# A hybrid decoder step on one core: x of the head groups and B brought to tokens on the partitions by VectorE's 32x32 transposes and a trip through DRAM

## The chip, the core and the metric

The kernel runs on one core of a Trainium2 chip. The metric is the device time of one execution in microseconds (us). The engines are TensorE (PE, with PEld for its weight loads), VectorE (DVE), ScalarE (ACT), GpSimd (POOL) and SyncE (SP, which here only issues DMAs). Each engine works through its own list of instructions in order.

## The reference

One step of a decoder layer with two parallel head groups, followed by a convolutional feed-forward part, for 256 prompt tokens and 64 sample tokens (8 sequences of 8):

```python
h = rms_norm(x, p["norm_mix_pre"])
proj = h @ p["w_in"]                       # columns: u | v | z | x,B,C | dt
gate_out, chunk_v = chunk_spatial_gate(a_u, a_v, ...)
ssm_out, new_ssm, new_ssm_conv = ssd_mixer(z, xbc, dt_raw, ...)
mix = jnp.concatenate([gate_out, ssm_out], axis=-1) @ p["w_out"]
x = x + rms_norm(mix, p["norm_mix_post"])
f, new_ffn_conv = conv_ffn(rms_norm(x, p["norm_ffn_pre"]), ...)
x = x + rms_norm(f, p["norm_ffn_post"])
```

The change lies in the state-space part (`ssd_scan`), which works on 32 heads of 64 values in four groups, a state of 128 values, and chunks of 128 tokens. With x, B, C after the convolution and silu:

```python
xdt = (x * dt[..., None])
cb = jnp.einsum("bctgn,bcsgn->bctsg", cc, bc)
y_diag = jnp.einsum("bctsgr,bcsgrp->bctgrp", cb[..., None] * decay, xdt)
states = jnp.einsum("bcsgn,bcsgr,bcsgrp->bcgrpn", bc, decay_states, xdt)
y_off = jnp.einsum("bctgn,bcgrpn,bctgr->bctgrp", cc, states_in, jnp.exp(da_cs))
y = y + d_skip[:, None] * xs
```

The sums over s in `y_diag` and `states` run over tokens, so x and B are needed with tokens on the partitions; the projection and the convolution leave them with channels on the partitions.

## The kernel before

All activations lie transposed: channels on the 128 partitions, the 320 tokens along the free axis (256 prompt, then 64 sample tokens). Every weight matrix is streamed once in slabs of 128x1024 float32 (512 KB). `slab` loads a slab on SP's queue (L118, `wraw`), ScalarE rounds it to `whi` (L124), VectorE computes the rest `wlo` (L125), and TensorE makes three products for each 128x128 block (L153 to L155: high by high, high by the low part of the activations, low by high), 24 products of 320 columns to a slab. `wraw`, `whi` and `wlo` have three buffers each.

Work between the slabs is written as generators: `project` (an input projection) and `chunk_out` (a part of the output projection) call `tick()` at slab edges, which takes the next step of the first generator in `bg`. A scheduler then decides the order of each engine's instructions from priorities and readiness; `first()` and `high_priority` raise a priority.

The order around the change: projections of v; then B (`conv_proj(B0, ...)` into `bT`), C (`cT`) and the first x (`heads_in(0)`); then four groups of the gate with `chunk_out` 0 to 3; then the pool `sd` opens and the state scan begins. It is run by `ssd(g)` for g = 0 to 3, beside `heads_in(g)`, `chunk_out` and `heads_out(g)`, whose evacuation first finishes `ssd(g)`. Inside `ssd(g)`:

- `load_state` brings the sample sequences' states (`st`, 256 KB each, six buffers) in on SP's queue; `load_sums` brings cumulated decays (`cs`, three buffers).
- `by_token` (L393) is a TensorE transpose of a 128x128 block of x or B into a PSUM bank. For the prompt it takes `xs[:, j]` for two chunks c; for the samples `fourfold` (L397) first copies 32 tokens four times beside each other on ScalarE, and the copy is transposed. B is treated likewise, once, before the first group (L775 to L786): prompt into `btok`, samples into `bsp` with a high and a low part.
- `times` (L824) multiplies the transposed x by dt into `xdt` (prompt and samples) or `xq` (samples with decay), reading PSUM.
- `decayed` (L830, POOL) gives `xde`, from which `s1_ps` (L876) is the state after the first chunk.
- `cb_ps` (L856 to L859) are the products of B and C, `yo_ps` (L887) those of C and the old states, `up_ps` (L904) the states' updates, `y_ps` (L983) the outputs, `fin_ps` (L1011) the last state.

## Time and profile before

| | us |
|---|---|
| runs, median of 3 | 1779.38 (1778.97 to 1780.19) |
| profiled execution, its span | 1779.7 |
| TensorE busy | 1770.5 |
| VectorE busy | 1168.0 |
| ScalarE busy | 819.5 |
| POOL busy | 273.5 |

The profiler names engines and lines: L393 is line 393 of the kernel. A group of instructions is shown as line, engine, operation, output <- inputs, partitions x elements and count, then busy time and the mean duration in ns, then the idle time of the engine just before and what ended it. A row of waits reads: who waited, for whom, us in total, times, the longest. A timeline row reads: start, duration, engine, line, operation. Matmuls are pipelined, so durations of neighbours overlap and TensorE's busy time does not say that it works at its peak.

### The profile page before, as it was taken

To read this page: it belongs to the slowest core of one execution; us is meant where nothing else is said; L and a number is where in the kernel's file an instruction comes from. 1 tells how busy PE (TensorE), PEld (TensorE's weight loads), DVE (VectorE), ACT (ScalarE), POOL (GpSimd) and SP (SyncE) were. 2 spreads that over 40 slices of the span, in tenths; PEclk is the share of its full clock that TensorE was granted. 3 is DMA by queue.
4 is the path that set the end of the run, shared out by engine and by line. 5 is a ranking of instruction groups with operands and counts; after the bars stand their busy time and mean duration, and the time that the engine had idled before them with its cause. 6 is when DMAs were issued, how large, how long until landed. Compare 5 with 4: busy or idle time off the path is not lost.

```text
span 1779.7 us, 30655 instructions
## 1 busy us (share of the span) xinstructions
PE 1770.5 (99%) x11933; PEld 1715.7 (96%) x11933; DVE 1168.0 (66%) x1999; ACT 819.5 (46%) x1195; POOL 273.5 (15%) x602
## 2 busy tenths in 40 slices
PE   9999999999999999999999999999999999999998
PEld 7789999999999998999999999999999999999998
DVE  7549764656977768677865464756656575656575
ACT  5434555334564547445545333343434343433445
POOL 1202200000331313103121011110102020101004
PEclk9999999999999999999999999999999999999999
DMA  7546645456665665554554545545545545454543
GB/s 260 163 148 177 189 128 154 153 153 188 216 190 190 181 207 168 168 171 145 180 156 146 157 149 151 155 148 152 157 144 156 150 150 155 150 150 155 147 154 107
DMA packets 214417, 289.91 MB, mean 163 GB/s; under 512 B 16384, under 2 KB 143744, under 8 KB 214080
## 3 DMA queue, kind: packets, MB, share of 16 engines
q1 hardware_dynamic: 202544, 268.74, 49.6%
q10 hardware_dynamic: 10016, 14.16, 2.2%
q0 software_dynamic: 1712, 5.05, 1.0%
q8 instruction: 94, 1.54, 0.4%
q14 instruction: 51, 0.42, 0.1%
HBM read 273.08 MB, written 14.82 MB: 162 GB/s over the span
## 4 chain that ended last, share of the span: by engine, by line
PE 97%; DVE 1%; ACT 0%; DMA 0%; issue 0%; POOL 0%; POOLq 0%; ACTq 0%; DVEq 0%
PE ps L153 19%; PE ps L155 19%; PE ps L154 19%; PE pd L153 10%; PE pd L155 10%; PE pd L154 10%; PE ps_v L144 7%; PE y_ps L983 1%; PE up_ps L904 0%; PE yo_ps L887 0%; PE sg L731 0%; PE xt_ps L393 0%; DMA cs<-dacs_d 0%; PE x1p L1278 0%; PE tsum L296 0%
## 5 line engine op out<-in xcount | busy, mean ns | idle before, releaser
L125 DVE TENSOR_TENSOR wlo<-wraw,whi 128x1024 fp32r<-128x1024 f32 (+1 forms) x476 | 582.5, 1224 | 432.4 <-ACT whi L124 430.1
L124 ACT CAST whi<-wraw 128x1024 fp32r<-128x1024 f32 (+1 forms) x475 | 494.8, 1042 | 729.9 <-PE ps L154 392.1
L153 PE MATMUL ps<-h_hi,whi 128*128 128x320 f32 x2268 | 704.0, 311 | 0.0
L154 PE MATMUL ps<-h_lo,whi 128*128 128x320 f32 x2268 | 702.7, 310 | 0.0
L155 PE MATMUL ps<-h_hi,wlo 128*128 128x320 f32 x2268 | 702.2, 310 | 0.0
L153 PEld LDWEIGHTS ps<-h_hi,whi 128*128 128x128 f32 x2268 | 426.2, 188 | 2.6 <-issue 1.6
L154 PEld LDWEIGHTS ps<-h_lo,whi 128*128 128x128 f32 x2268 | 426.3, 188 | 0.7
L155 PEld LDWEIGHTS ps<-h_hi,wlo 128*128 128x128 f32 x2268 | 426.2, 188 | 0.0
L155 PE MATMUL pd<-fhi,wlo 128*128 128x320 f32 x704 | 218.2, 310 | 0.0
L153 PE MATMUL pd<-fhi,whi 128*128 128x320 f32 x704 | 218.2, 310 | 0.0
L154 PE MATMUL pd<-flo,whi 128*128 128x320 f32 x704 | 218.2, 310 | 0.0
L153 PE MATMUL pd<-ohi,whi 128*128 128x320 f32 x448 | 139.4, 311 | 0.0
L155 PE MATMUL pd<-ohi,wlo 128*128 128x320 f32 x448 | 138.7, 310 | 0.0
L154 PE MATMUL pd<-olo,whi 128*128 128x320 f32 x448 | 138.7, 310 | 0.0
L153 PEld LDWEIGHTS pd<-fhi,whi 128*128 128x128 f32 x704 | 132.1, 188 | 0.0
L154 PEld LDWEIGHTS pd<-flo,whi 128*128 128x128 f32 x704 | 132.1, 188 | 0.0
L155 PEld LDWEIGHTS pd<-fhi,wlo 128*128 128x128 f32 x704 | 132.1, 188 | 0.0
L1180 POOL COPY ptf<-pad 128x2 f32<-128x2 f32 x88 | 21.0, 239 | 603.7 <-DVE pad L1168 603.0
L249 DVE TENSOR_TENSOR acc_ffn<-acc_ffn,pd 128x320 f32<-128x320 f32 (+1 forms) x161 | 77.5, 482 | 37.8 <-PE pd L155 36.5
L153 PEld LDWEIGHTS pd<-ohi,whi 128*128 128x128 f32 x448 | 84.1, 188 | 1.4 <-issue 1.0
L154 PEld LDWEIGHTS pd<-olo,whi 128*128 128x128 f32 x448 | 84.1, 188 | 0.3
L155 PEld LDWEIGHTS pd<-ohi,wlo 128*128 128x128 f32 x448 | 84.1, 188 | 0.1
(328 smaller groups left out, 1867.9 us busy)
## 6 DMA issues: line engine op xcount, KB each, us to landing
wraw<-in_ffn_w_up SPq DMA_DIRECT2D x176, 512.0 KB, 3.7
wraw<-in_w_in SPq DMA_DIRECT2D x140, 512.0 KB, 3.8
wraw<-in_ffn_w_down SPq DMA_DIRECT2D x88, 512.0 KB, 3.4
wraw<-in_w_out SPq DMA_DIRECT2D x64, 512.0 KB, 3.4
st<-in_state_ssm SPq DMA_DIRECT2D x32, 256.0 KB, 3.9
out_ssm_state_sample<-st ACTq DMA_DIRECT2D x30, 256.0 KB, 3.4
cs<-dacs_d SPq DMA_DIRECT2D x16, 320.0 KB, 4.7
xr<-in_xT SPq DMA_DIRECT2D x4, 640.0 KB, 4.0
```

The costliest lines, as they stand in the source:

```text
L124: rounded[:] = [act.copy(hi, raw).ins]
L125: dve.tensor_tensor(out=lo, in0=raw, in1=hi.bitcast(F32), op=ALU.subtract)
L144: made = pe.matmul(out, xi, w[g][wi], start=first and begins, stop=last and ends)
L153: pe.matmul(ps, whi, xhi, start=first, stop=False)
L154: pe.matmul(ps, whi, xlo, start=False, stop=False)
L155: return pe.matmul(ps, wlo, xhi, start=False, stop=last).ins
L249: added_last[:] = [dve.tensor_tensor(out=acc[:, nb, ts], in0=acc[:, nb, ts], in1=ps[:, ts], op=ALU.add).ins]
L983: pe.matmul(ps[64 * i:64 * i + 64, cols], w(hl), x(hl, m, cpx), tile_position=(0, 64 * i), **flags)
L1180: pool.tensor_copy(ptf[:, k, :], pad[:, 256:258])
```

## The change

No TensorE transposes remain for x and B. `to_tokens` takes a tile with channels on the partitions and, for each part of the tokens (128, 128, 64), lets VectorE transpose its 32x32 blocks (two instructions of 128x512 and one of 128x256 for a tile), then ScalarE's queue issues four writes of it, one for each 32 partitions, into a DRAM buffer with tokens as rows: 12 writes for a tile, five tiles (B and four x), 60 writes. The columns of such a row are in the order (i j f), i the block of partitions, j the tile's block, f the 32 channels.

Reads come back on SP's queue: two of 256 KB for the prompt and eight of 64 KB for the samples (`fourfold` now reads the same 32 rows four times) for each tile, 50 in all. They land in `room()`, tiles that share the three buffers of `cs`. `in_order` turns the columns' order while B is copied to `btok` and `bsp`; `times` does it while multiplying by dt, in two instructions (r = 0, 1) where one stood, reading SBUF.

B and the first x are turned right after their projections. x of group g+1 is turned at the end of `ssd(g)`, behind its products of y in the code. The loads of the states come after the reads of the prompt's x, the products of B and C now stand ahead of everything else that TensorE does in a group, and `state_of_prompt` holds what stood after the first samples' x.

```diff
--- before.py
+++ after.py
@@ -339,6 +339,8 @@
 
     dacs_d = dr.tile([NH, NT + NS], F32, name="dacs_d")
     tot_d = dr.tile([NH, NB], F32, name="tot_d")
+    b_d = dr.tile([NT, 512], F32, name="b_d")
+    x_d = [dr.tile([NT, 512], F32, name=f"x_d{i}") for i in range(4)]
 
 
     hp = ctx.enter_context(tc.tile_pool(name="hp", bufs=1))
@@ -388,14 +390,25 @@
 
     TOK = ((0, P), (P, P), (NP, NS))
 
-    def by_token(ps, x, c):
-
-        pe.transpose(ps, x[:, P * c:P * c + P], ident)
-
-    def fourfold(out, x, i):
-
-        act.copy(out.rearrange("p k (q t) -> p k q t", q=4), x[:, :, NP + 32 * i:NP + 32 * i + 32].unsqueeze(2).to_broadcast([P, 4, 4, 32]))
+    def to_tokens(room, x, rows):
+
+        for o, n in TOK:
+            t = room(o)[:, :4 * n].rearrange("p (s j f) -> p s j f", j=4, f=32)
+            dve.transpose(out=t, in_=x[:, :, o:o + n].rearrange("p j (s t) -> p s j t", t=32))
+            for i in range(4):
+                act.dma_start(rows[o:o + n, P * i:P * i + P].rearrange("(s t) f -> t s f", t=32),
+                              t[32 * i:32 * i + 32].rearrange("p s j f -> p s (j f)"))
+
+    def fourfold(out, rows, i):
+
+        src = rows[NP + 32 * i:NP + 32 * i + 32]
+        for q in range(4):
+            sp.dma_start(out[32 * q:32 * q + 32], src)
         return out
+
+    def in_order(ap):
+
+        return ap.rearrange("p (i j f) -> p j i f", j=4, f=32)
 
     with ExitStack() as mctx:
         op = mctx.enter_context(tc.tile_pool(name="op", bufs=1))
@@ -749,9 +762,12 @@
             conv_proj(B0, 16, lambda j: bT[:, j, :], rooms[0])
             conv_proj(C0, 20, lambda j: cT[:, j, :], rooms[1])
             bg.append(tasks)
+            turned = op.tile([P, 4, NT], F32, tag="xs", name="turned", bufs=2).rearrange("p j n -> p (j n)")
+            to_tokens(lambda o: turned[:, 4 * o:], bT, b_d)
             x0 = heads_in(0, rooms[0])
             finish(normed)
             uf = gate_up(0)
+            to_tokens(lambda o: turned[:, 4 * o:], x0, x_d[0])
             for g in range(4):
                 res = []
                 mix = gate_mix(g, uf, res)
@@ -772,18 +788,20 @@
             cb, cms = shared[:, :NT + NS], shared[:, NT + NS:].rearrange("p (b i) -> p b i", b=NB)
             pool.tensor_copy(cb[:NS, :NS], ident[:NS, :NS])
             pool.tensor_copy(cb[NS:, NT:], ident[NS:, NS:])
-            for c in range(4):
-                ps = misc("bt_ps")
-                b4 = bT if c < 2 else fourfold(sd.tile([P, 4, P], F32, tag="xde", name="b4", bufs=2), bT, c - 2)
-                for g in range(4):
-                    by_token(ps[:, P * g:P * g + P], b4[:, g], c if c < 2 else 0)
-                if c < 2:
-                    act.copy(btok[:, c, :], ps)
-                else:
-                    b = bsp[:, c - 2]
-                    act.copy(b, ps)
-                    for rs in (slice(32, 64), slice(96, P)):
-                        dve.tensor_tensor(out=b[rs], in0=ps[rs], in1=b[rs].bitcast(F32), op=ALU.subtract)
+            def room():
+                return sd.tile([P, 2, NT], F32, tag="cs", name="xt", bufs=3).rearrange("p i n -> p (i n)")[:, :512]
+
+            for c in range(2):
+                b = room()
+                sp.dma_start(b, b_d[P * c:P * c + P])
+                act.copy(btok[:, c, :].rearrange("p (j i f) -> p j i f", j=4, f=32), in_order(b))
+            for c in range(2):
+                b4 = fourfold(room(), b_d, c)
+                b = bsp[:, c]
+                act.copy(b.rearrange("p (j i f) -> p j i f", j=4, f=32), in_order(b4))
+                for rs in (slice(32, 64), slice(96, P)):
+                    h = b[rs].rearrange("p (j i f) -> p j i f", j=4, f=32)
+                    dve.tensor_tensor(out=h, in0=in_order(b4[rs]), in1=h.bitcast(F32), op=ALU.subtract)
 
             def by_head(ap):
                 return ap.rearrange("p (h d) -> p h d", d=64)
@@ -816,13 +834,15 @@
                     sp.dma_start(cs, dacs_d[h0 + 2 * j:h0 + 2 * j + 2, o:o + NT].unsqueeze(0).broadcast_to([P, 2, NT]))
                     return cs
 
-                sts = [load_state(i) for i in range(3)]
-
                 xdt = sd.tile([P, 3, 512], F32, tag="xdt", name="xdt", bufs=1)
-                def times(out, ps, c, at=slice(0, P), h=slice(0, 8)):
-                    n = h.stop - h.start
-                    dve.tensor_tensor(out=by_head(out), in0=by_head(ps),
-                                      in1=dt[at, c, h0 + h.start:h0 + h.stop].unsqueeze(2).to_broadcast([at.stop - at.start, n, 64]), op=ALU.mult)
+                def times(out, x, c, at=slice(0, P), h=slice(0, 8)):
+                    n, m = at.stop - at.start, (h.stop - h.start) // 2
+                    to = out.rearrange("p (j r i f) -> p r j i f", j=m, r=2, i=2)
+                    of = x.rearrange("p (r i j f) -> p r j i f", r=2, i=2, j=4)[:, :, h.start // 2:h.stop // 2]
+                    by = dt[at, c, h0 + h.start:h0 + h.stop].rearrange("p (j r) -> p r j", r=2)
+                    for r in range(2):
+                        dve.tensor_tensor(out=to[:, r], in0=of[:, r],
+                                          in1=by[:, r].unsqueeze(2).unsqueeze(3).to_broadcast([n, m, 2, 32]), op=ALU.mult)
 
                 xsp = sd.tile([P, 2, 512], F32R, tag="xsp", name="xsp", bufs=1)
                 def decayed(i, c):
@@ -832,25 +852,31 @@
                     return xde
 
                 def x_of_samples(i):
-                    ps = misc("xt_ps")
-                    x4 = fourfold(sd.tile([P, 4, P], F32, tag="xde", name="x4", bufs=2), xs, i)
-                    for j in range(4):
-                        by_token(ps[:, P * j:P * j + P], x4[:, j], 0)
+                    x4 = fourfold(room(), x_d[g], i)
                     xq = sd.tile([P, 512], F32, tag="xde", name="xq", bufs=2)
-                    times(xq, ps, 3 + i)
+                    times(xq, x4, 3 + i)
                     act.copy(xsp[:, i], xq)
                     dve.tensor_tensor(out=xsp[64:, i], in0=xq[64:], in1=xsp[64:, i].bitcast(F32), op=ALU.subtract)
                     for r in range(2):
                         at = slice(64 - 64 * r + 32 * i, 96 - 64 * r + 32 * i)
-                        times(xdt[at, 2, 256 * r:256 * r + 256], ps[at, 256 * r:256 * r + 256], 2, at, slice(4 * r, 4 * r + 4))
-
-                for c in range(2):
-                    ps = misc("xt_ps")
-                    for j in range(4):
-                        by_token(ps[:, P * j:P * j + P], xs[:, j], c)
-                    times(xdt[:, c, :], ps, c)
-                    if c == 0:
-                        x0d = decayed(0, 0)
+                        times(xdt[at, 2, 256 * r:256 * r + 256], x4[at], 2, at, slice(4 * r, 4 * r + 4))
+
+                s1 = sd.tile([P, 512], F32, tag="s1", name="s1", bufs=1)
+
+                def x_of_prompt(c):
+                    x = room()
+                    sp.dma_start(x, x_d[g][P * c:P * c + P])
+                    times(xdt[:, c, :], x, c)
+
+                def state_of_prompt(x0d):
+                    ps = misc("s1_ps")
+                    pe.matmul(ps, btok[:, 0, bs], x0d, start=True, stop=True)
+                    act.copy(s1, ps)
+
+                x_of_prompt(0)
+                x0d = decayed(0, 0)
+                x_of_prompt(1)
+                sts = [load_state(i) for i in range(3)]
                 ps = misc("cb_ps")
                 for c in range(2):
                     pe.matmul(ps[:, P * c:P * c + P], bT[:, g, P * c:P * c + P], cT[:, g, P * c:P * c + P],
@@ -872,10 +898,7 @@
                 x_of_samples(0)
                 yield
 
-                ps = misc("s1_ps")
-                pe.matmul(ps, btok[:, 0, bs], x0d, start=True, stop=True)
-                s1 = sd.tile([P, 512], F32, tag="s1", name="s1", bufs=1)
-                act.copy(s1, ps)
+                state_of_prompt(x0d)
 
                 ps_yo = misc("yo_ps")
 
@@ -1002,6 +1025,8 @@
                             products(j - 1)
                         yield
 
+                if g < 3:
+                    to_tokens(lambda o: room(), x_of[g + 1], x_d[g + 1])
                 x1d = decayed(1, 1)
                 pool.tensor_tensor(out=by_head(s1), in0=by_head(s1),
                                    in1=dec[:, 2, h0:h0 + 8].unsqueeze(2).to_broadcast([P, 8, 64]), op=ALU.mult)
```

## The prediction

> **What bounds the kernel now.** First the page of the profile: busy times, and the chain that ended last by engine.
>
> ```profile
> PE 1770.5 (99%) x11933; PEld 1715.7 (96%) x11933; DVE 1168.0 (66%) x1999; ACT 819.5 (46%) x1195; POOL 273.5 (15%) x602
> ...
> PE 97%; DVE 1%; ACT 0%; DMA 0%; issue 0%; POOL 0%; POOLq 0%; ACTq 0%; DVEq 0%
> ```
>
> TensorE is busy for 99% of the span and makes up 97% of the chain. An average hides stages, so next the busy times by stretches (columns: us, then PE, PEld, DVE, ACT and POOL busy with instruction counts, clock, DMA share, GB/s), the last row the whole state-scan part that the change touches:
>
> ```profile
> 465.00:486.00 21.00, 21.00 (x147) 19.52 (x146) 20.92 (x37) 10.96 (x19) 8.05 (x14) 1.00 0.80 251
> ...
> 420.00:740.00 320.00, 318.85 (x2325) 298.74 (x2324) 246.57 (x418) 184.72 (x341) 80.85 (x101) 1.00 0.61 192
> ```
>
> There too TensorE, at a granted clock of 1.00, idles 1.2 us of 320, even in the stretch where VectorE has no gap (20.92 of 21.00). So a TensorE instruction taken away is time taken away, unless a new wait fills it. How far the others run ahead is in the waits of ScalarE, and in three casts of one quiet stretch:
>
> ```profile
> ACT whi L124 <- PE ps L154: 392.1, 186, 4.5
> ...
> 138.78 1.05 ACT L124 CAST whi<-wraw 128x1024 fp32r<-128x1024 f32 x1 [2.43 <-PE ps L154]
> 142.30 1.05 ACT L124 CAST whi<-wraw 128x1024 fp32r<-128x1024 f32 x1 [2.47 <-PE ps L154]
> ```
>
> ScalarE's cast of a weight slab mostly waits until TensorE gives a buffer back, not the other way round. One slab lasts 3.52 us (142.30 - 138.78). With three whi/wlo buffers the split runs up to two slabs, about 7.0 us, ahead of the products; this is the cover for everything that the change adds to ScalarE, VectorE and SP. With three raw buffers behind those, SP can issue the load of slab i once slab i-6 is multiplied and slab i-3 is cast and subtracted.
>
> **The gain.** The transposes' groups (ns minimum/median/maximum, first and last start), and TensorE's timeline around sixteen of them:
>
> ```profile
> L393 PE MATMUL xt_ps<-ident,xs x32: 272/272/273, 436.3 to 689.1; 128*128 128x128 f32 x32
> L393 PE MATMUL xt_ps<-ident,x x32: 271/272/273, 442.4 to 700.5; 128*128 128x128 f32 x32
> L393 PE MATMUL bt_ps<-ident,bT x8: 272/272/273, 428.1 to 429.4; 128*128 128x128 f32 x8
> L393 PE MATMUL bt_ps<-ident,b x8: 272/273/330, 435.3 to 436.2; 128*128 128x128 f32 x8
> ...
> 434.89 0.31 PE L153 MATMUL ps<-h_hi,whi 128*128 128x320 f32 x1
> 435.04 0.31 PE L154 MATMUL ps<-h_lo,whi 128*128 128x320 f32 x1
> 435.30 1.18 PE L393 MATMUL bt_ps<-ident,b 128*128 128x128 f32 x8
> 436.31 1.04 PE L393 MATMUL xt_ps<-ident,xs 128*128 128x128 f32 x8
> 437.10 0.39 PE L155 MATMUL ps<-h_hi,wlo 128*128 128x320 f32 x1
> ```
>
> 80 transposes go. Each shows 272 ns, but they overlap: an ordinary product starts 0.15 us after the one before (435.04 - 434.89), and around the sixteen it is 437.10 - 435.04 = 2.06 us, so 1.91 us for sixteen or 0.119 us each. 80 x 0.119 = 9.5 us. That is the value I take, since spacing is what delays the next product.
>
> [...]
>
> **What comes in, and where it lies.** In the compiled order of the changed kernel no other TensorE instruction is added or dropped. The rest, with the nearest rows:
>
> ```profile
> L125 DVE TENSOR_TENSOR wlo<-wraw,whi 128x1024 fp32r<-128x1024 f32 x74 | 94.4, 1276 | 28.0 <-ACT whi L124 27.8
> L249 DVE TENSOR_TENSOR acc_mix<-acc_mix,pd 128x320 f32<-128x320 f32 x52 | 25.0, 481 | 7.8 <-PE pd L155 7.4
> ...
> L824 DVE TENSOR_TENSOR xdt<-xt_ps,dt 128x512 f32<-128x512 f32 x8 | 5.2, 683 | 0.0
> ...
> L830 POOL TENSOR_TENSOR xde<-xdt,dec 128x512 f32<-128x512 f32 x8 | 8.8, 1104 | 69.9 <-DMA cs<-dacs_d 55.9 <-DVE xdt L824 11.1 <-issue 3.0
> ...
> L962 ACT ACT_TABLE_LOAD x4 | 5.1, 1283 | 0.1
> ...
> 473.81 0.94 ACTq L911 DMA_DIRECT2D out_ssm_state_sample<-st  x2
> ```
>
> VectorE: five tiles of two transposes 128x512 and one 128x256. No transpose on VectorE stands in the trace; by width one lies between the 128x320 row (0.48) and the 128x1024 row (1.28), and the 128x512 row is 0.68, so I take 0.68 + 0.68 + 0.48 = 1.8 us a tile, 9 us in all (bounds 5 x 1.44 = 7 and 5 x 3.84 = 19). The products with dt split into halves (`times`, two for one): at 0.48 for a half against 0.68 whole some 0.3 us more for each of 16 wide ones, the 32 narrow ones less; about 7 us more. 16 us on 1168 of 1779.7; in the scan part VectorE has 320 - 246.6 = 73 us of gaps. I cost it at nothing: the lead of two slabs hides it. Without that cover a tile's 1.8 us would hold a slab's wlo.
>
> ScalarE: ten copies 128x512 (L397) go, which I count as nothing since they could only help. 60 writes are issued on it at 0.94/2 = 0.47 us, 28 us, twelve for each tile (5.6 us a burst). The new order also has 35 loads of function tables for 26: 9 x 1.28 = 11.5 us. Some 40 us on 819.5; in the scan part up to 29 (three bursts, nine loads) of the 320 - 184.7 = 135 us of gaps. Queued behind a write that waits are the casts, and TensorE waits for those after 7.0 us.
>
> SP: 50 reads more, at the same 0.47 us 24 us of a queue that mostly waits for buffers; the weight loads are behind them. The reads sit between weight loads, mostly two to five to a slab, 0.9 to 2.4 us of 3.52. DMA: 3.3 MB written and 5.2 MB read more, 8.5 MB on 289.9 MB at a share of 0.61; no row speaks for that as a bound.
>
> **The new wait.** Before, `xdt` came out of TensorE directly. Now every group's x goes VectorE, write, read, VectorE, POOL, and only then the product of `state_of_prompt` may start; behind it on TensorE stand the products with the states and all slab products. The landing times (KB, us to landing):
>
> ```profile
> st<-in_state_ssm SPq DMA_DIRECT2D x32, 256.0 KB, 3.9
> out_ssm_state_sample<-st ACTq DMA_DIRECT2D x30, 256.0 KB, 3.4
> cs<-dacs_d SPq DMA_DIRECT2D x16, 320.0 KB, 4.7
> ...
> 500.52 1.69 PE y_ps L983 x32
> 505.95 0.86 PE fin_ps L1011 x2
> ...
> 438.15 0.68 PE cb_ps L856 x4
> ```
>
> From the compiled order I count how many slab products lie between the place that lets a read go and the first product that needs it. The read of group 1 follows the load of slab 141: after the slab that frees it, cast 1.05 + subtraction 1.28 + two issues 0.9 + landing 3.9 + two halves 1.0 + POOL 1.1 = 9.2 us. TensorE has meanwhile 55 slab products (2.29 x 3.52 = 8.1) and 2.8 of y, fin and cb products, 10.9 us: 1.7 to spare. Group 2 has 13.8 us (three slabs, 3.2 of others); there the four writes that the read needs come last: cast 1.05, three issues 1.4, landing 3.4, then 6.5 for the read and what follows it, 12.3 us, 1.5 to spare. Group 3 has 11.9 (2.46 slabs, 3.2 of others) against 9.2, 2.7 to spare. In group 0 the x is written long before, but the state loads now stand behind the reads of B and x: the first comes 2.3 + 0.9 + 3.9 = 7.1 us after its slab is free, its product after 39 slab products (5.7) and one of 0.4: 1.0 late.
>
> The spare is eaten by what delays the casts and writes, at most a burst of 5.6: then 1.0 + 3.9 + 4.1 + 2.9 = 11.9 us of waits; at the least nothing, if landings are faster than the medians. I take 4.5, well under half, because the first read needs only four of the twelve writes.
>
> **Sum.** 1779.7 - 9.5 + 4.5 = 1774.7 in the profile's time; the runs' median (1779.38) lies 0.3 below its span: 1774.4.
>
> **The rivals.**
> - Clean gain: all four trips hidden. For it: in the compiled order these products of groups 0 and 3 come 1.5 to 3.3 slabs later than before, and TensorE's idle in the scan part is 1.2 us now. 1779.7 - 9.5 = 1770.2; if their busy time went as the timeline shows it for the sixteen, (1.18 + 1.04) / 16 x 80 = 11.1, it is 1768.6.
> - The trip gives the gain back: the upper bound of the waits, 1779.7 - 9.5 + 11.9 = 1782.1, no change. For it: the margins are 1.5 to 2.7 us and the reads land under a DMA share of 0.6. Against: three groups have spare at median landings.
> - VectorE becomes the bound: in a stretch like 465 to 486 it has no room, and a tile's 1.8 us and 1.4 of split products could pass straight to TensorE at the three tiles made in the scan part: 1779.7 - 9.5 + 9.6 = 1779.8. Against: TensorE stayed full in that stretch, and the lead is larger than 3.2 us. [...]
> - Slower: ScalarE is held by its own writes. Each write waits on one of eight semaphores that the DMAs share in turn, so on the DMA eight before, which may be a weight load just issued. A burst with its issues (5.6) and two rounds of landings at 3.9 lasts 13.4 us with casts queued between; past 7.0 us TensorE starves, 6.4 us a burst. With three bursts in the scan part: 1779.7 - 9.5 + 19.2 = 1789.4. For it: the order shows such waits on more than half of the writes. Against: casts stand between the writes, and a load issued eight DMAs earlier has mostly landed. It decides once a burst holds ScalarE for two slabs.
> - That the change does nothing, its transposes being hidden now, is excluded by the 1.91 us row.
>
> **Chances and range.** A difference of 0.2% (3.6 us, 1775.8 to 1783.0) is what a measurement can tell. Forecast (waits of 1.5 to 5.5) 0.34, clean 0.22: faster 0.56. Gain given back 0.21, VectorE 0.05: same 0.26. ScalarE held 0.18: slower. The range from 1768.5 (clean, whole busy time) to 1783.0 leaves out most of the last; the forecast's own range is 1771.5 to 1775.8.
>
> **What would show it.** Right: no L393 groups; PE busy lower by about 9 to 11 us; waits on PE before the `state_of_prompt` and state products of 0.5 to 3 us each; VectorE's transposes near 0.7 us; casts that still wait mostly for PE. Wrong: PE idle over 8 us in 420 to 740 at casts (ScalarE held), at wlo (VectorE), or at the products behind x (the trip longer than 9.2 us); or a gap in 150 to 260, where B and the first x are written, which I cost at nothing.

## The result and the profile after

The changed kernel took 1800.12 us in the median (1796.80 to 1800.91, four runs), the kernel before beside it 1779.47: a ratio of 1.011, 95% interval 1.0099 to 1.0122. It is 20.6 us slower, outside the range of the prediction. First the busy times and the chain that ended last on the page of the changed kernel:

```profile
PE 1774.5 (99%) x11853; PEld 1714.5 (95%) x11853; DVE 1188.5 (66%) x2046; ACT 826.5 (46%) x1194; POOL 270.8 (15%) x602
...
PE 91%; DVE 4%; DMA 2%; issue 2%; ACT 1%; POOL 0%; ACTq 0%; DVEq 0%; POOLq 0%; SPq 0%
```

The 80 transposes are gone (11853 for 11933), yet TensorE counts 4 us more of busy time, and its share of the chain fell from 97% to 91%. The stretches (PE, PEld, DVE, ACT, POOL busy, clock, DMA share, GB/s) show where:

```profile
465.00:486.00 21.00, 17.53 (x102) 16.06 (x101) 17.68 (x30) 7.66 (x12) 5.88 (x6) 0.92 0.69 218
420.00:740.00 320.00, 304.53 (x2109) 280.18 (x2107) 249.61 (x435) 172.10 (x299) 74.23 (x96) 0.98 0.68 208
```

In the scan part TensorE idles 15.5 us of 320 (1.2 before). Its waits in the scan, the last of which ends just behind 740, as engine, tile and line, what it waited for, us in total, times, longest:

```profile
PE up_ps L927 <- DVE xsp L859: 8.7, 6, 2.0
PE yo_ps L910 <- DMA st<-in_state_ssm: 5.3, 3, 2.0
PE s_ps L873 <- POOL xde L850: 1.8, 2, 1.4
PE y_ps L1006 <- DVE cs L995: 1.3, 3, 0.8
```

Together 17.1 us. The place that the prediction priced, the prompt's state (`s_ps`), is the small one; the large ones are the products of the samples' x (`up_ps`) and of the states (`yo_ps`). Before, the same list had two rows, 1.0 us in all:

```profile
PE up_ps L904 <- DVE xsp L842: 0.8, 2, 0.6
PE y_ps L983 <- DVE cs L972: 0.2, 1, 0.2
```

The first of these two is worth noticing: the samples' x was already just in time before anything was changed. VectorE's part, the transposes and the products with dt (mean ns after the comma), of the changed kernel and then of the one before:

```profile
L397 DVE STREAM_TRANSPOSE xt<-xs 128x512 f32<-128x512 f32 x6 | 4.2, 706 | 0.1
...
L844 DVE TENSOR_TENSOR xdt<-xt,dt 32x128 f32<-32x128 f32 x32 | 14.0, 466 | 3.1 <-DMA xt<-x_d 2.7
...
L844 DVE TENSOR_TENSOR xdt<-xt,dt 128x256 f32<-128x256 f32 x16 | 8.8, 593 | 1.3 <-DMA xt<-x_d 1.1
L844 DVE TENSOR_TENSOR xq<-xt,dt 128x256 f32<-128x256 f32 x16 | 8.8, 580 | 0.1
```

```profile
L824 DVE TENSOR_TENSOR xdt<-xt_ps,dt 32x256 f32<-32x256 f32 x16 | 6.7, 420 | 0.3
L824 DVE TENSOR_TENSOR xq<-xt_ps,dt 128x512 f32<-128x512 f32 x8 | 5.5, 684 | 1.5 <-PE xt_ps L393 1.5
L824 DVE TENSOR_TENSOR xdt<-xt_ps,dt 128x512 f32<-128x512 f32 x8 | 5.2, 683 | 0.0
```

The products cost 31.6 us for 17.4, and VectorE itself now stands 3.8 us waiting for reads. One of the six waits, in the changed kernel's timeline (start, us, engine, line, work; in brackets the idle time before and its cause):

```profile
458.55 1.43 SPq L406 DMA_DIRECT2D xt<-x_d  x3
...
463.70 1.05 DVE L440 SCALAR_TENSOR_TENSOR cv<-pad,prm,cv 128x344 f32<-128x344 f32 x2
...
465.07 1.77 DVE L125 TENSOR_TENSOR wlo<-wraw,whi 128x1024 fp32r<-128x1024 f32 x1
466.77 1.28 DVE L844 TENSOR_TENSOR xq<-xt,dt 128x256 f32<-128x256 f32 x1
...
468.37 0.41 DVE L844 TENSOR_TENSOR xq<-xt,dt 128x256 f32<-128x256 f32 x1
...
468.82 0.62 ACT L858 CAST xsp<-xq 128x512 fp32r<-128x512 f32 x1 [3.84 <-DVE xq L844]
...
470.34 0.69 DVE L859 TENSOR_TENSOR xsp<-xq,xsp 64x512 fp32r<-64x512 f32 x1
...
471.09 0.50 PE L927 MATMUL up_ps<-xsp,bm 128*128 128x512 f32 x1 [1.45 <-DVE xsp L859]
```

The three reads, the last of the four for this product, had landed by 462.6 (landing times of the trace). The halves of `xq` start only 4.2 us later, because they stand among other work (`cv`, `wlo`) of a VectorE that has hardly a gap there, and every link behind them (cast, subtraction, product) is that much later. A last view: behind two of the waits for a state load and one for the samples' x the granted clock falls.

```profile
480.00:482.00 2.00, 1.56 (x5) 1.14 (x6) 0.30 (x1) 0.00 (x0) 0.00 (x0) 0.73 0.94 335
482.00:484.00 2.00, 2.00 (x8) 1.81 (x8) 1.37 (x2) 0.00 (x0) 0.00 (x0) 0.50 0.77 295
484.00:486.00 2.00, 2.00 (x15) 2.00 (x14) 1.27 (x2) 0.00 (x0) 0.00 (x0) 0.92 0.85 223
480.00:500.00 20.00, 19.37 (x116) 17.64 (x117) 15.10 (x27) 10.66 (x16) 2.85 (x6) 0.91 0.92 295
620.00:640.00 20.00, 17.86 (x105) 15.26 (x106) 14.49 (x21) 8.37 (x18) 6.39 (x7) 0.91 0.87 269
720.00:740.00 20.00, 16.37 (x92) 14.74 (x90) 12.40 (x20) 7.38 (x14) 2.54 (x2) 0.91 0.86 255
```

The granted clock is 0.50 for 3.41 us three times, from 480.92, 627.70 and 733.51 us, and 1.00 just before and after; each costs (1 - 0.91) x 20 = 1.8 us, 5 in all, counted as busy.

To see where time comes and goes, I took the start of every slab product (10964 in each trace) and subtracted that of the same product in the kernel before. Columns: when that product ran in the kernel before (us); values: later (+) or earlier (-).

| kernel | 420 | 450 | 500 | 680 | 700 | 720 | 780 |
|---|---|---|---|---|---|---|---|
| changed | -2.1 | -7.8 | +2.1 | +10.7 | +6.1 | +8.6 | +17.8 |
| e10_one_of_four | -2.7 | -5.6 | -5.5 | -6.3 | -8.0 | -3.3 | -3.3 |
| e14_first_clean | -2.5 | -5.5 | -4.2 | -3.9 | -3.9 | -3.9 | -3.9 |
| e18_all_but_last | -2.1 | -5.0 | -4.3 | -4.7 | -4.7 | -4.7 | -4.7 |
| e19_last_only | -2.0 | -2.0 | -2.1 | -2.1 | -3.8 | +2.3 | +2.3 |
| e8_halved_before | -2.0 | -2.0 | -2.0 | -0.6 | -0.6 | +2.7 | +2.7 |
| e13_whole_products | -1.2 | -6.8 | +2.7 | +5.9 | +1.3 | +3.0 | +10.5 |

Some 2 us of lead at 420 have nothing to do with the change: the profiled execution of the kernel before had a stretch of lower clock of its own between 240 and 250 us (1.6 us by this row of it), which the others had not.

```profile
240.00:250.00 10.00, 8.96 (x50) 8.36 (x49) 4.79 (x10) 6.96 (x10) 2.45 (x4) 0.84 0.48 144
```

After 780 us nothing changes. So the changed kernel lost 17.8 + 2.1 = 19.9 us, all in the scan.

### The profile page after: what moved, and what is told of

Read it like the earlier page. It is cut to its first block, busy times and chain, and to the rows that moved or that the text cites. A ratio compares the mean times of both kernels' runs of the same rounds, so it can differ in the third digit from the quotient of the medians.

```text
span 1798.6 us, 30673 instructions
## 1 busy us (share of the span) xinstructions
PE 1774.5 (99%) x11853; PEld 1714.5 (95%) x11853; DVE 1188.5 (66%) x2046; ACT 826.5 (46%) x1194; POOL 270.8 (15%) x602
## 4 chain that ended last, share of the span: by engine, by line
PE 91%; DVE 4%; DMA 2%; issue 2%; ACT 1%; POOL 0%; ACTq 0%; DVEq 0%; POOLq 0%; SPq 0%
PE ps L153 18%; PE ps L154 17%; PE ps L155 17%; PE pd L153 9%; PE pd L154 9%; PE pd L155 9%; PE ps_v L144 7%; DVE wlo L125 1%; PE y_ps L1006 1%; DMA out_ssm_state_sample<-st 1%; DMA st<-in_state_ssm 1%; PE sg L744 0%; ACT whi L124 0%; DVE xq L844 0%; PE up_ps L927 0%
```

## The experiments

Medians; the ratio is to the kernel before on the same chip. The scheduler orders every edited kernel anew, so each difference holds the edit and a new order together. I counted in the traces how many of TensorE's 793 instructions beside slab products and transposes of x and B have another number of slab products ahead of them than in the kernel before: 18 in e14_first_clean, 19 in e18_all_but_last, 36 in e19_last_only, 55 in e10_one_of_four (by at most 13 slab products, 1.9 us), 326 in the changed kernel.

| kernel | us | ratio, 95% interval |
|---|---|---|
| e1_states_first | 1799.4 | 1.0107 (1.0092 to 1.0122) |
| e2_samples_pe | 1789.0 | 1.0053 (1.0038 to 1.0068) |
| e3_b_only | 1781.1 | 1.0004 (0.9994 to 1.0013) |
| e6_writes_beside | 1784.4 | 1.0024 (1.0014 to 1.0035) |
| e4_early_write | 1807.6 | 1.0150 (1.0132 to 1.0167) |
| e7_samples_pe_early | 1793.0 | 1.0072 (1.0054 to 1.0090) |
| e8_halved_before | 1783.5 | 1.0018 (1.0009 to 1.0027) |
| e9_all_eased | 1828.7 | 1.0269 (1.0252 to 1.0287) |
| e10_one_of_four | 1781.7 | 1.0014 (1.0004 to 1.0024) |
| e11_old_x | 1797.2 | 1.0101 (1.0085 to 1.0117) |
| e12_samples_earlier | 1797.1 | 1.0094 (1.0079 to 1.0109) |
| e13_whole_products | 1791.4 | 1.0063 (1.0048 to 1.0078) |
| e14_first_clean | 1778.2 | 0.9989 (0.9979 to 0.9998) |
| e15_natural | 1800.1 | 1.0113 (1.0096 to 1.0130) |
| e16_natural_samples_pe | 1791.9 | 1.0059 (1.0044 to 1.0074) |
| e17_early_two | 1785.1 | 1.0030 (1.0021 to 1.0039) |
| e18_all_but_last | 1778.1 | 0.9985 (0.9976 to 0.9994) |
| e19_last_only | 1784.7 | 1.0025 (1.0016 to 1.0034) |

### Is it the order in SP's queue?

```diff
-                sts = [load_state(i) for i in range(3)]   # behind x_of_prompt(1)
+                sts = [load_state(i) for i in range(3)]   # ahead of x_of_prompt(0)
```

> The changed kernel with the state loads of a group put back ahead of its reads of x. My theory now: TensorE, which takes its work in order, waits in the scan at three places: at the products of the states with the samples' x (8.7 us on its list of waits), at the products of C with the states, whose loads stand behind the reads of B and x (5.3 us), and behind the longer of these waits its granted clock falls to half for about 4 us, some 2 us each. By it the 5.3 us go with two or three of the drops: 1800.1 - 5.3 - 4 = about 1790. Rival 1, the reads of x come later by what the state loads take, and the wait only moves: 1798 to 1804. Rival 2, VectorE's added work sets the pace: the waits for the samples' x stay and the place of the loads hardly matters, 1797 to 1801. Rival 3, the issue of writes on ScalarE or the added traffic: unchanged, 1799 to 1801.

1799.4: the wait only moved. On TensorE's list of this kernel:

```profile
PE up_ps L928 <- DVE xsp L861: 11.4, 6, 4.4
PE yo_ps L911 <- DMA st<-in_state_ssm: 3.4, 3, 2.0
```

The two rows sum to 14.8 us (14.0 in the changed kernel): what the state loads gain, the samples' x loses. My first theory missed that.

```diff
+                x_of_samples(0)          # ahead of sts, was one step later
-                    if i == 0: x_of_samples(1)
+                x_of_samples(1)          # where x_of_samples(0) was
```

> The changed kernel with the reads and products of the samples' x one step earlier in the program: the first with the prompt's, the second where the first stood. Nothing else changes. If the waits at the products of states and x (8.7 us) come from reads that stand too late in SP's order for the four reads, two halves, cast and subtraction behind them, most of them go with a drop or two of the clock: 1786 to 1792. If the reads only push the state loads and weight loads back as e1_states_first showed, the wait moves: 1797 to 1803. If VectorE has no room for them earlier, xdt of the prompt and the splits are late: above 1803.

1797.1, the second answer; the 3.0 us less than the changed kernel are not clear of noise (the intervals of the ratios overlap). Again most of the wait moves between the same two rows (5.9 and 6.2 us).

### Is it the trip's landing?

```diff
-                    x4 = fourfold(room(), x_d[g], i)
+                    x4 = fourfold(room(), x_d[0], i)
-                    sp.dma_start(x, x_d[g][P * c:P * c + P])
+                    sp.dma_start(x, x_d[0][P * c:P * c + P])
```

> The changed kernel, but every group reads x of group 0, which was written long before; the writes of the other groups stay and nothing waits for them. It takes away the wait of the reads for the writes alone (8.6 + 2.9 us on SP's list), leaving reads, queue places and VectorE's work. If the trip's landing is what is late, as the prediction's rival had it (the upper bound of its waits was 11.9 us): 1788 to 1793. If what is late is the reads' place in SP's queue behind weight loads, and VectorE's work behind them: 1796 to 1801.

1797.2, the second answer: 2.9 us of some 20 go by the medians, 1.6 by the ratios, whose intervals overlap. The samples' products wait as before (trace of a run of 1802.1 us):

```profile
PE up_ps L927 <- DVE xsp L859: 10.4, 6, 2.6
```

So what the edit takes away of the landing is a small part of the loss. It does not take all: SP's waits for writes of x in the scan fall from 11.5 to 5.3 us, since the writes still hold the rooms into which the reads go.

```diff
                 x_of[g] = heads_in(g)
+                to_tokens(lambda o: room(), x_of[g], x_d[g])   # and not at the end of ssd(g - 1)
```

> The changed kernel with x of the next group turned and written right behind its projection in place of the end of the group before. My theory: part of the lateness of the samples' x is SP standing at the reads until the writes have landed (8.6 + 2.9 us on SP's list of waits in the scan); with the writes done long before, the three late groups lose 1 to 2 us of wait each and one drop of the clock: 1792 to 1796. Rival, SP is held by the state loads, which wait for the stores of the states before them (37.1 us): unchanged, 1798 to 1802. Rival, the burst only meets other work, whose casts it delays: 1800 to 1806.

1807.6, worse, and a little beyond the last answer. ScalarE's list in 420 to 760 us of this kernel shows a row that the changed kernel hasn't:

```profile
ACT whi L124 <- DMA x_d<-xt: 13.7, 5, 3.9
```

Casts of weights now wait for writes of x: the mechanism of the prediction's slower rival, but here, not in the changed kernel.

### Which part of the trip?

```diff
-                    x4 = fourfold(room(), x_d[g], i)
+                    x4 = copies(..., xs, i)            # ScalarE's copy, then four transposes, as before
-                    times(xq, x4, 3 + i)
+                    times_ps(xq, ps, 3 + i)
```

> The changed kernel with the samples' x alone back on TensorE's transposes (32 of the 80 return, 32 of the 50 reads and 16 of the 60 writes go). My theory: the transposes cost 32 x 0.119 = 3.8 us, the waits for the samples' x fall from 8.7 to about 1, half of the waits for state loads goes with the reads ahead of them (2.6), and about two drops of the clock (4): 1800.1 + 3.8 - 7.7 - 2.6 - 4 = about 1790. Rival, VectorE's transposes and the halved products of the prompt: most of the loss stays, 1798 to 1804. Rival, the prompt's trip is the dear one: 1800 or above.

1789.0, as forecast: the samples' x is the dearer half of the change. With its 3.8 us of transposes back, its trip (reads, writes and halves together) costs 1800.1 - 1789.0 + 3.8 = 14.9 us.

> The samples' x on TensorE (as in e2_samples_pe), with the state loads first and the prompt's x turned and written right behind its projection. 48 of 80 transposes stay away, 5.7 us. In e2_samples_pe (1789.0) the waits left are at the samples' x in groups 1 to 3 (6.6 us) with two drops of the clock (about 4). My theory: they come from the burst of eight writes on ScalarE and four transposes on VectorE at a group's end, which e6_writes_beside priced at 4.2; with the burst moved away they go, 1789.0 - 6.6 - 4 = about 1778. Rival, the prompt's reads and halved products hold VectorE and SP: 1785 to 1790. Rival, the moved burst costs the same elsewhere: 1786 to 1792.

1793.0, just above the third answer: moved to another place, the burst of writes cost no less there (the edit is those of e4_early_write and e1_states_first on top of e2_samples_pe).

> Only B by the trip through DRAM, x wholly on TensorE as before (16 of the 80 transposes are gone; the state loads stand ahead of x's work as before). My theory: B is written some 150 us before it is read and nothing waits: 1779.5 - 16 x 0.119 = 1777.6. Rival, the ten reads of B in SP's queue delay the first state loads and weight slabs: a wait of 2 to 4 us and a drop of the clock, 1780 to 1784.

1781.1, no difference, where 1777.6 was forecast. Even B, written long before, gains nothing (the edit takes x out of the trip).

```diff
+            to_tokens(lambda o: turned[:, 4 * o:], bT, b_d)
+            to_tokens(lambda o: turned[:, 4 * o:], x0, x_d[0])
+                if g < 3: to_tokens(lambda o: room(), x_of[g + 1], x_d[g + 1])
```

> The kernel before with the change's VectorE transposes and its 60 writes beside it, which nothing reads: all 80 transposes stay on TensorE, no read, no halved product. My theory: all this lies in the gaps of VectorE and ScalarE, 1779.5 to 1782. Rival, ScalarE held by its own writes, or their traffic: 1788 to 1800. Rival, VectorE full at the tiles made in the scan (3 x 1.8 us of transposes passed on): 1783 to 1786.

1784.4, the last answer: the ratio prices the writes and VectorE's transposes at 4.3 us, though nothing reads them. The price holds the rooms too: the tiles written out take the three buffers of `cs`, and SP's loads of the decays wait 6.8 us for the writes. The samples' products wait 3.7 us in it:

```profile
PE up_ps L921 <- DVE xsp L859: 3.7, 3, 1.9
```

```diff
+                    for r in range(2):
+                        s, o = slice(64 * n * r, 64 * n * (r + 1)), h0 + h.start + n * r
+                        dve.tensor_tensor(out=by_head(out[:, s]), in0=by_head(ps[:, s]), ...)
```

> The kernel before with each product of x and dt in two halves over the heads, and nothing else: the price of the halves on VectorE alone. My theory: at 0.48 for 0.68 us, 14 us more of VectorE's time over the scan meet the one stretch where it has no gap (465 to 486) and the samples' x comes 0.3 to 0.6 us later in each half: 1781 to 1784. Rival, all of it lies in gaps: 1779 to 1780.5. Rival, VectorE is the bound and the whole passes on: 1790 or more.

1783.5, the first answer: the halves alone cost 3.2 us by the ratio; they make VectorE's products 20.1 us long for 17.4. The table shows the places: 1.4 us in groups 1 and 2, then 3.3 us between 700 and 720, a wait of 1.8 us for a state load with a granted clock of 0.96 over 700 to 740, (1 - 0.96) x 40 = 1.6 us.

```diff
-                    for r in range(2):
-                        dve.tensor_tensor(out=to[:, r], in0=of[:, r], ...)
+                    dve.tensor_tensor(out=by_head(out), in0=by_head(x)[:, h], ...)
```

> The changed kernel with every product of x and dt in one instruction over all heads, as before the change, on the columns as they lie (the order of the channels in x is left unmended). In the kernel before, the halves alone cost 3.7 us (e8_halved_before). If that adds up with the rest: 1796 to 1797. If in the changed kernel VectorE, full where TensorE waits, is the bound there, more: 1788 to 1793. If the waits are for the reads alone: 1799 to 1801.

1791.4, the second answer: with whole products 8.7 us go. VectorE's products take 23.8 us for the 31.6 of the changed kernel, the samples' wait is half as long, and the granted clock over 420 to 740 is 0.99 (0.98 in the changed kernel); one of the three drops is left, with slab products of 0.47 us for 0.31 from 728.75 us on:

```profile
PE up_ps L923 <- DVE xsp L855: 4.3, 6, 1.3
...
L840 DVE TENSOR_TENSOR xdt<-xt,dt 32x256 f32<-32x256 f32 x16 | 11.7, 732 | 0.3
```

So VectorE's added work is a large part of the loss. It is not the price of halving alone: a narrow half lasts 0.28 us in e8_halved_before and 0.47 in the changed kernel, where it also turns the columns, which e13_whole_products leaves out. Whole products with the channels in order came next.

```diff
-            in_=x[:, :, o:o + n].rearrange("p j (s t) -> p s j t", t=32)
+            in_=x[:, :, o:o + n].rearrange("p j (t s) -> p s j t", t=32)
-                act.dma_start(rows[o:o + n, P * i:P * i + P].rearrange("(s t) f -> t s f", t=32), ...)
+                act.dma_start(rows[o:o + n].rearrange("(t s) c -> t (s c)", t=32).rearrange("t (m i f) -> t m i f", i=4, f=32)[:, :, i, :], ...)
```

> The whole change, with the columns mended on the way: the transposes take every fourth (samples: every second) token and the writes lay x and B down in their own order of channels, in runs of 128 bytes in place of 512, so that each product with dt is one instruction again. e13_whole_products, which left the order unmended, took 1791.4. Theory: the halves are dear because VectorE has no gap where TensorE waits, and the shorter runs only lengthen writes that e11_old_x showed to matter little (2.9 us with no wait for them at all): 1791 to 1795. Rival, short runs and strided transposes cost as much as the halves: 1797 to 1803.

1800.1, the rival. By the groups of this kernel a transpose that takes every fourth token lasts 1.11 us for 0.71:

```profile
L397 DVE STREAM_TRANSPOSE xt<-xs 128x512 f32<-128x512 f32 x6 | 6.6, 1107 | 0.0
```

Its samples' products hardly wait any more:

```profile
PE up_ps L923 <- DVE xsp L855: 1.7, 2, 1.2
```

Yet the time is that of the changed kernel. Others wait in their place: the products of the states 6.7 us for their loads, those of the prompt's state 4.0, of which the list puts 2.2 down to a write of x; and products still slow down in three places (slab products of 0.47 us for 0.31 from 640.73 and from 745.47 us, two products of the prompt's state that take 1.84 us at 714.42). The writes in short runs land no later (24 of 64 KB: 3.0 us in the median, 3.1 in the changed kernel). So the wait for the samples' x does not set the time by itself. Which part the strided transposes, the short runs and the new order have in taking back the 8.7 us was not separated.

> e15_natural with the samples' x on TensorE: 48 of 80 transposes away, no halves, the rooms and reads of the samples gone. e2_samples_pe took 1789.0 with the prompt's products halved. Theory: the halves of the prompt cost 2 to 4 us of that: 1785 to 1787. What is left over the kernel before is then the prompt's trip and the writes. Rival, the halves of the prompt, which come first in a group, meet VectorE's gaps: 1788 to 1790.

1791.9: the same with the samples on TensorE, no better than e2_samples_pe (1789.0).

```diff
+                    if g == 0:          # by the trip; else four transposes and times_ps
+                        x = room()
+                        sp.dma_start(x, x_d[g][P * c:P * c + P])
```

> The trip for B and for the prompt's x of the first group alone, both written some 150 us before they are read, in their own order of channels; the rest on TensorE, the state loads first. 24 transposes away, 2.9 us. If a trip that is long over costs nothing but its reads: 1777 to 1778, below the kernel before. If, as e3_b_only (1781.1) hints, the reads in SP's queue ahead of the first state loads cost what is gained: 1779.5 to 1782.

1785.1, worse than both answers. Its samples' products wait 4.9 us, though the samples' x is on TensorE as before; a trip that is long over is not free either.

```diff
-            sp.dma_start(out[32 * q:32 * q + 32], src)
+            pool.dma_start(out[32 * q:32 * q + 32], src)
-                    x4 = fourfold(room(), x_d[g], i)
+                    x4 = fourfold(sd.tile([P, 512], F32, tag="xde", name="x4", bufs=2), x_d[g], i)
```

> The changed kernel, all 80 transposes away, with four easings: x written right behind its projection, the state loads first, the reads of x on POOL's queue in place of SP's, the samples' rooms no longer taken from the decays' three buffers but from those of xde. My theory: the queue, the rooms and the burst made the trip late, so most of the 20.6 us goes: 1778 to 1786. Rival, VectorE's own work (transposes and halved products, some 25 us more in the scan than before) is what holds the samples' x: 1790 to 1798. Rival, POOL's queue is held by its own waits, and x is later still: above 1800.

1828.7, the third answer (the edits of e4_early_write and e1_states_first are in it too). POOL's list has waits behind ScalarE and VectorE of up to 46.8 us, and the reads stand in that list: the samples' products wait 15.4 us. Which of the four easings costs how much was not separated.

### Was the gain there at all?

```diff
-                    for j in range(4):
-                        by_token(ps[:, P * j:P * j + P], xs[:, j], c)
+                    by_token(ps[:, :P], xs[:, 0], c)      # one block stands for four; likewise x4 and B
```

> The gain by itself: the kernel before, of whose 80 transposes only the first of each four is made and read four times over; 60 are left out, so x and B have one block of channels in place of four. Nothing else comes in. By the spacing of 0.119 us the prediction's gain of 9.5 us for 80 is 7.1 us for 60: 1779.8 - 7.1 = 1772.7, which would show that the gain was sized rightly and that the change lost it elsewhere. Rival, the gain itself was mis-sized, since the chain through VectorE to the samples' products then ends earlier on TensorE and waits instead: 1776 to 1779.

1781.7 for 1780.0. Sixty transposes less and nothing added, and the kernel is no faster. In the table it runs ahead as forecast (2.9 us from 420 to 450, where 24 are left out: 24 x 0.119 = 2.9), and keeps most of it until 700; then it falls back:

```profile
PE yo_ps L890 <- DMA st<-in_state_ssm: 2.0, 1, 2.0
PE up_ps L907 <- DVE xsp L846: 1.7, 2, 1.0
```

> As e10_one_of_four, but only B and the first group have one transpose in place of four: 24 are left out, the other three groups are as before. In e10_one_of_four the 60 left out put TensorE's slab products ahead by what was forecast until the last group, and there a wait for state loads (2.0 us), one for the samples' x and a drop of the clock took it back. Theory: what is left out in the first group meets no wait and is kept, 24 x 0.119 = 2.9: about 1777. Rival, the later groups are paced by loads and stores that do not move with TensorE, and it waits there for what it is ahead: 1779 to 1781.5.

1778.2, between the two answers: 2.0 us faster by the ratio (0.4 to 3.7). In the table 3.0 is gained by 450 and 1.4 kept at the end.

> As e10_one_of_four, with the last group's transposes put back: 48 of 80 left out. Against the slab products of the kernel before, e10_one_of_four's trace was 3.7 us further ahead at 680 us than at 420 and lost it in the last group. Theory: what the first three groups gain is kept but for the two waits seen there: 1779.9 - 3.7 = 1776.2. Rival, that place in the trace was chance and the gain is given back wherever the loads or VectorE come next: 1779 to 1782.

1778.1, between the two answers: 2.7 us faster (1.1 to 4.3), with 48 left out, 5.7 forecast by spacing; 3.7 was expected from the trace.

> Only the last group has one transpose in place of four, 12 left out; B and the other groups as before. Theory: in e10_one_of_four's trace the last group gained 1.9 and lost 4.9 (waits for the samples' x and for state loads, and a drop of the clock), so leaving these twelve out makes the kernel slower: about 1782. Rival, the loss there came from the groups before it: 1779.9 - 1.4 = 1778.5.

1784.7, slower as forecast and by more: twelve transposes taken away, with the new order that comes of it, make the kernel 4.4 us slower by the ratio. TensorE is 1.8 us ahead at 700 and 4.3 behind at 720. From this kernel's timeline:

```profile
705.27 0.34 SPq L809 DMA_DIRECT2D st<-in_state_ssm  x1
...
706.81 0.94 ACTq L917 DMA_DIRECT2D out_ssm_state_sample<-st  x2
...
708.00 2.15 ACTq L917 DMA_DIRECT2D out_ssm_state_sample<-st  x3
...
711.70 0.62 PE L893 MATMUL yo_ps<-st,cb_cms 128*32 128x256 f32 x2
...
712.67 0.34 SPq L809 DMA_DIRECT2D st<-in_state_ssm  x1
...
715.76 0.63 PE L893 MATMUL yo_ps<-st,cb_cms 128*32 128x256 f32 x6 [3.44 <-DMA st<-in_state_ssm]
...
706.00:712.00 6.00, 6.00 (x41) 5.55 (x39) 5.48 (x10) 1.34 (x2) 0.00 (x0) 1.00 0.88 294
```

and from that of the kernel before:

```profile
704.74 6.32 SPq L809 DMA_DIRECT2D st<-in_state_ssm  x2
...
707.17 0.34 ACTq L911 DMA_DIRECT2D out_ssm_state_sample<-st  x1
...
714.95 0.64 PE L887 MATMUL yo_ps<-st,cb_cms 128*32 128x256 f32 x8
...
706.00:712.00 6.00, 6.00 (x43) 5.20 (x42) 5.11 (x9) 2.25 (x4) 2.08 (x2) 1.00 0.67 250
```

Before, the last state load was issued at 710.7 (704.74 + 6.32 less one issue) and its product came at 714.95, with no wait. Now TensorE is there at 711.70, but the load, whose buffer a store of a state must free first, is issued only at 712.67. That store is not late: it is issued at 706.81, before at 707.17. But it lands after 5.8 us for 3.5, in a stretch in which five stores follow each other and the DMA engines are busy for 0.88 of the time (0.67 before; the share is the last figure but one of the rows 706 to 712). That the crowd slows the store is argued, not tried. TensorE waits 3.4 us, and behind it the granted clock is 0.71 over 5 us, in the stretches of e19_last_only:

```profile
715.00:720.00 5.00, 4.24 (x22) 3.83 (x23) 2.10 (x3) 0.00 (x0) 3.06 (x2) 0.71 0.35 107
```

## Why the prediction was wrong

The step that failed first is the sentence "So a TensorE instruction taken away is time taken away, unless a new wait fills it." Its first half rested on 1.2 us of idle in 320. The size of the gain was right: in the trace of the kernel before the 80 transposes take 8.4 us from their starts to the next, 9.4 with the changes to them, for 9.5 in the sum. But the scan's own products (`up_ps`, `yo_ps`) got their data just in time from VectorE, SP and the stores, so TensorE was full without being the only bound. e10_one_of_four and e19_last_only show it without any trip, though with a new order: what is taken away can turn into a wait at a later product whose data does not come earlier, and the wait can cost more than was taken away. e14_first_clean and e18_all_but_last keep a part.

The second is the term of 4.5 us for the new waits, with 11.9 as its bound. Measured are 17.1 us less the 1.0 before. The prediction followed the prompt's x to `s_ps`, which came to 1.8, and gave the landing of the trip the price; e11_old_x, which takes away half of SP's waits for it, gains 2.9 by the medians, not clear of noise. It did not follow the samples' x, four reads, two halves, a cast and a subtraction long, to `up_ps` (8.7 us), nor the state loads of the later groups (5.3 with group 0's).

The third is the cost of VectorE's work at nothing. The transposes were sized well (0.71 for 0.68 us); the products came to 14.2 us more instead of 7. But the cover was the wrong one: two slabs of lead cover the weights' splits, not the scan's chain, which runs through the same VectorE without such a lead. Plain halves cost 3.2 us in the kernel before; halves that turn the columns cost 8.7 in the changed one. That was the prediction's VectorE rival in kind, which priced it at 9.6 and thought it unlikely.

Right were the quiet of 150 to 260 us (no loss until 420), and that ScalarE is not held: its casts still wait mostly for TensorE.

```profile
ACT whi L124 <- PE ps L154: 55.8, 23, 5.6
ACT whi L124 <- PE pd L154: 39.4, 16, 7.7
```

The slower rival thus named the wrong engine, and no case reached 1800. Not in the sum at all was the half clock, 5 us. The 19.9 us lost in the scan then are -9.4 (transposes) + 16 (waits) + 5 (clock), which is 11.6; the other 8.3 are spread over the products of the scan. Order would explain most of it: TensorE changes from slab products to `y_ps`, `up_ps` and `yo_ps` 47 times where it did 27 times (counted in the two traces). Two `y_ps` products alone hold the slab products up for 0.45 us, 32 in one go for 1.78, so a change costs an estimated 0.25 to 0.4 us, and twenty of them 5 to 8. Why the scheduler mixes them more was not tried, nor the old order with the new work.

Open is also which part of e6_writes_beside's 4.3 us is ScalarE's issues, which VectorE's transposes and which the shared rooms. No version with the trip beat the kernel before. e14_first_clean and e18_all_but_last put what free transposes could give at 2 to 3 us.

## What to carry to other kernels

A busy share of 99% says that an engine has no gaps, not that it alone sets the time: look for products that wait a few tenths of a microsecond already, for they show that other chains end at the same moment. Before paying for a removal with reads, writes and other engines' work, leave the instructions out and see what a free removal would give; here 60 left out gave nothing, and 48 gave 2.7 us. When work goes into an engine that also carries a chain to the bound engine, ask whether the lead that you count on covers that chain or only the stream beside it.

## What the runs showed of the hardware

In e10_one_of_four, behind the wait of 2.0 us shown above, the granted clock was 0.83 over 705 to 715, (1 - 0.83) x 10 = 1.7 us on top of the wait.

```profile
705.00:715.00 10.00, 7.96 (x45) 6.81 (x44) 4.43 (x7) 1.04 (x1) 3.06 (x2) 0.83 0.70 231
```

But in e7_samples_pe_early one of 2.55 us brought no drop (its timeline, and the stretch that holds the wait, with a clock of 1.00):

```profile
636.60 0.63 PE L928 MATMUL yo_ps<-st,cb_cms 128*32 128x256 f32 x6 [2.55 <-DMA st<-in_state_ssm]
```

```profile
620.00:660.00 40.00, 35.32 (x229) 32.65 (x230) 27.60 (x50) 19.39 (x35) 10.37 (x9) 1.00 0.65 208
```

Two waits of nearly one length differ as well: behind one of 1.81 us in e8_halved_before the clock drops (0.96 over 700 to 740), behind one of 1.85 us in e6_writes_beside it does not (1.00 over 515 to 525).

```profile
716.12 0.63 PE L889 MATMUL yo_ps<-st,cb_cms 128*32 128x256 f32 x6 [1.81 <-DMA st<-in_state_ssm]
700.00:740.00 40.00, 38.19 (x271) 35.40 (x270) 23.94 (x39) 16.39 (x29) 10.68 (x9) 0.96 0.55 156
```

```profile
521.49 0.47 PE L921 MATMUL up_ps<-xsp,bm 128*128 128x512 f32 x1 [1.85 <-DVE xsp L859]
515.00:525.00 10.00, 8.14 (x60) 6.54 (x59) 9.45 (x12) 5.99 (x14) 7.39 (x7) 1.00 0.47 156
```

And in the kernel before the row of 240 to 250 shows 0.84 with 1.04 us of idle time in all. So the length of a wait does not tell by itself, in these runs, whether a drop follows; what decides it was not shown.
